# One hybrid decoder block on one core: where weight casts are issued, and how u and y pass through DRAM

## The chip, the core and the metric

The kernel runs on one core of one Trainium2 chip. A core has four compute engines with an instruction queue each: TensorE (PE in the profile; its weight loads are PEld), VectorE (DVE), ScalarE (ACT) and GpSimd (POOL). SyncE (SP) computes nothing here and issues most of the DMAs; ScalarE issues some too. Each queue is worked off in order: an instruction that waits holds up everything behind it on the same engine. The metric is the device time of the whole kernel in microseconds (us). Three runs of the kernel before gave 1589.52, 1594.77 and 1595.97 us, a median of 1594.77.

## The reference, cut to what matters

One layer, 1024 tokens, width 1024, all float32:

```
u = rms_norm(h) ; proj = u @ w_in -> u_ssm, q, k, v, f_logit, gate_logits
y_ssm = gelu(s5_ssm(u_ssm, ...))          # 32 groups of 16 channels, 64 states each
out_a = glu(y_ssm @ w_glu)
out_b = forgetting_attention(q, k, v, f_logit + b_forget) @ w_fox_o      # 8 heads of 64
h = h + (gate_a * out_a + gate_b * out_b) @ w_mix_out
h = h + memory_cross_attention(rms_norm(h), rms_norm(mem), ...)
h = h + (silu(f_a) * f_b) @ w_ffn_out ; out = rms_norm(h)
```

The recurrence of `s5_ssm` is worked in blocks of 8 time steps, so that a group's data has rows of (step within the block, channel of the group), and 128 columns, one for each block.

## The kernel before, in words

Every float32 product is made as three matmuls of a split operand: a rounded copy `hi` (a cast on ScalarE, line 174) and the remainder `lo` (a subtraction on VectorE, line 175). Weights take this way: a DMA into a `raw` buffer (two buffers), the cast into a `whi` buffer and the subtraction into a `wlo` buffer (four each). A `raw` buffer comes free when its subtraction is done, a `whi` buffer when the last matmul that reads it is done. The order of instructions on the engines is not the order of the lines: a scheduler works the program through at build time with a model of durations, and may take an instruction as soon as that model has its inputs and its buffers ready. `B.tc.issue_after(ins)` is the means against it: the instructions of the block that run on the engine of `ins` come behind `ins` in that engine's queue.

The stages, with the times of the profile before:

- **Input** (0 to 111 us): norms, the memory's keys and values, and the projection of `u_ssm` (`ssm_in`, `ssm_out`) in four quarters of 128 channels. `ssm_out` (line 418) copies a quarter to `us`, 128 channels by 8 steps by 128 blocks, and stores it to `u_d` with one DMA for each of its 8 groups (lines 424 and 425).
- **Gates and recurrence** (111 to 327 us, `stage_ssm`): 32 steps `gate(j, h)` of 24 matmuls with a sigmoid on ScalarE, a store to `gate_d` that ScalarE issues (line 462), and the weights of the next gates by `wblock`. Between them, for each quarter q: `turn_weights` (transposes, two copies `F` on ScalarE, seven small DMAs `Ts` <- `W`), `states` (the load of `xg` from `u_d`, line 1346, 16 matmuls of `xg` with `F`, the scan on VectorE), `toeplitz` (one copy `Tt` <- `Ts` on ScalarE, line 1340, placed behind a sigmoid), `out` (16 matmuls, gelu, the split into `yh` and `yl`) and `store` (line 1403: 16 DMAs of 16 partitions each, which bring y to channel rows in `y_d`).
- **Values and first projections** (327 to 396 us): `Fox.prepare_v` loads and splits four blocks of the v weights; `values_of_v` makes v. `project(h)` has a `load` for the q and k weights of head h (two DMAs of 256-byte rows, the cast and the subtraction, lines 1530 to 1543), 16 `part`s of three matmuls, and `evac`.
- **Attention** (396 to 611 us): 8 heads of 12 units (`scores`, an exponential, `values_hi`, `values_lo`). Side work hangs on the units: the parts of head h+2, the row maxima of head h+1, and at unit 5 the `load` of head h+3 (line 1740). In head 6 stand the loads of y from `y_d` (`load_y`), in head 7 the loads of the first `w_glu` weights and their products.
- **Tail** (611 us to the end): the GLU, the mixing projection, cross-attention and the FFN.

## Time and profile before

| | us |
|---|---|
| three runs, median (lowest to highest) | 1594.77 (1589.52 to 1595.97) |
| the profiled execution, its own time | 1596.93 |
| its span, from the first to the last instruction | 1594.9 |
| PE busy in that span | 1537.0 |
| DVE busy | 1021.1 |
| ACT busy | 650.5 |
| POOL busy | 250.1 |

How to read the profile: its first part gives each engine's busy time, the second 40 slices of the span, the fourth the chain of work that ended last. The other views quoted below are answers of the same trace. In a view of stretches, each row has the stretch, its length, the busy time of each engine with the number of its instructions, the TensorE clock that was granted (1.00 is full speed), the share of time in which the DMA engines were busy, and what they moved in GB/s. In a timeline, each row has a start, a duration, the engine, the line, the operation, its output and input, how many instructions were merged, and in brackets how long the engine sat idle before it and what ended that. A row of SPq or ACTq is an instruction that issues a DMA, not the transfer.

### The profile page before, as it was taken

Reading aid. Unit: us, or ns where it says so; the run is one execution under the profiler, and the core shown is the slowest. Engines: PE = TensorE matmul, PEld = TensorE weight load, DVE = VectorE, ACT = ScalarE, POOL = GpSimd, SP = SyncE. Lnnn points to the kernel's source line nnn. Section 1 sums busy time; section 2 is a strip of 40 time slices with the busy share of each in tenths; the row PEclk is TensorE's granted clock in tenths of the full one; section 3 lists DMA queues with packets and bytes.
Section 4 is the critical chain, followed back from the end, with each engine's and each line's share of the span. In section 5 each row is a group of like instructions: output and inputs, shape, how many; then the busy total and the mean of one; then the engine's idle time right before and its main releaser. Section 6 shows DMA issues by size and latency. Waiting matters only on the chain.

```text
span 1594.9 us, 20583 instructions
## 1 busy us (share of the span) xinstructions
PE 1537.0 (96%) x7313; PEld 1263.9 (79%) x7313; DVE 1021.1 (64%) x1850; ACT 650.5 (41%) x1173; POOL 250.1 (16%) x339
## 2 busy tenths in 40 slices
PE   7799999999899999999999989999999999999997
PEld 6588888798677768888888778888888888788886
DVE  6657545345587876766555687776667776565455
ACT  6323434323466653223335564333333333344342
POOL 2026654200121222210002200010000000000001
PEclk8899999999899999999999999999999999999999
DMA  7747455641321526457402186555544444796642
GB/s 265 127 80 135 117 135 98 112 78 24 54 54 49 153 58 201 146 159 268 160 24 97 53 276 232 161 166 160 167 158 152 157 161 152 270 392 224 190 157 106
DMA packets 204278, 236.45 MB, mean 148 GB/s; under 512 B 36984, under 2 KB 133080, under 8 KB 204176
## 3 DMA queue, kind: packets, MB, share of 16 engines
q1 hardware_dynamic: 197552, 219.42, 47.9%
q10 hardware_dynamic: 6624, 15.73, 2.6%
q8 instruction: 57, 0.93, 0.3%
q14 instruction: 45, 0.37, 0.1%
HBM read 161.40 MB, written 71.66 MB: 146 GB/s over the span
## 4 chain that ended last, share of the span: by engine, by line
PE 78%; DVE 7%; DMA 6%; issue 4%; ACT 3%; SPq 1%; POOL 1%; DVEq 0%; POOLq 0%; ACTq 0%
PE mm L858 14%; PE mm L164 7%; PE mm L165 7%; PE mm L166 7%; PE pv L858 7%; PE mm L995 4%; PE sc L858 3%; PE sc L164 3%; PE sc L166 3%; PE sc L165 3%; PE sc L995 3%; PE pv L995 3%; DMA raw<-in_w_in_dram 2%; PE misc L995 1%; DMA xt<-in_x_dram 1%
## 5 line engine op out<-in xcount | busy, mean ns | idle before, releaser
L175 DVE TENSOR_TENSOR wlo<-raw,whi 128x1024 fp32r<-128x1024 f32 (+2 forms) x121 | 130.2, 1077 | 168.4 <-ACT whi L174 167.4
L174 ACT CAST whi<-raw 128x1024 fp32r<-128x1024 f32 (+2 forms) x124 | 112.3, 910 | 225.0 <-DMA raw<-in_w_ffn_in_dram 54.8
L164 PE MATMUL mm<-uh,whi 128*128 128x512 f32 x344 | 138.5, 403 | 0.0
L166 PE MATMUL mm<-uh,wlo 128*128 128x512 f32 x344 | 136.5, 397 | 0.0
L165 PE MATMUL mm<-ul,whi 128*128 128x512 f32 x344 | 136.2, 396 | 0.0
L175 DVE TENSOR_TENSOR ol<-or,oh 128x1024 fp32r<-128x1024 f32 x73 | 89.3, 1223 | 70.9 <-ACT oh L174 69.7
L174 ACT CAST oh<-or 128x1024 fp32r<-128x1024 f32 x73 | 76.8, 1053 | 104.3 <-PE mm L995 35.2
L890 POOL TENSOR_TENSOR g<-a,c 128x512 f32<-128x512 f32 x22 | 35.5, 1613 | 394.8 <-ACT a L889 394.8
L166 PEld LDWEIGHTS mm<-uh,wlo 128*128 128x128 f32 x344 | 65.7, 191 | 13.4 <-DVE wlo L175 0.2
L1625 POOL TENSOR_TENSOR pl<-pf,ph 128x512 fp32r<-128x512 f32 (+1 forms) x32 | 37.3, 1166 | 245.3 <-DVE ph L1624 154.6
L164 PEld LDWEIGHTS mm<-uh,whi 128*128 128x128 f32 x344 | 65.9, 192 | 12.1
L165 PEld LDWEIGHTS mm<-ul,whi 128*128 128x128 f32 x344 | 65.8, 191 | 11.5
L193 POOL TENSOR_TENSOR r<-ms,mhalf 128x1 f32<-128x1 f32 x26 | 15.1, 581 | 356.0 <-DVE ms L189 345.5
L1622 ACT ACTIVATE pf<-sc 128x512 f32<-128x512 f32 (+1 forms) x96 | 46.4, 489 | 52.7 <-DVE sc L1618 32.5
L858 PE MATMUL pv<-S3h,we 128*128 128x512 f32 x176 | 58.1, 389 | 0.0
L995 PE MATMUL mm<-ol,oh 128*128 128x512 f32 x106 | 41.3, 389 | 0.0
L995 PE MATMUL mm<-oh 128*128 128x512 f32 x106 | 41.2, 389 | 0.0
L995 PE MATMUL mm<-oh,ol 128*128 128x512 f32 x106 | 41.2, 389 | 0.0
L1628 DVE TENSOR_TENSOR pl<-pf,ph 128x512 fp32r<-128x512 f32 (+2 forms) x64 | 35.7, 558 | 8.4 <-ACT ph L1627 7.0
L164 PE MATMUL sc<-uh,whi 128*128 128x512 f32 x104 | 40.8, 393 | 0.0
L164 PE MATMUL mm<-yh,whi 128*128 128x512 f32 x104 | 40.8, 392 | 0.0
L165 PE MATMUL mm<-yl,whi 128*128 128x512 f32 x104 | 40.6, 390 | 0.0
(581 smaller groups left out, 4545.6 us busy)
## 6 DMA issues: line engine op xcount, KB each, us to landing
or<-c_d SPq DMA_DIRECT2D x77, 256.0 KB
raw<-in_w_in_dram SPq DMA_DIRECT2D x22, 512.0 KB
wo<-in_w_ffn_out_dram SPq DMA_DIRECT2D x22, 512.0 KB
c_d<-g SPq DMA_DIRECT2D x44, 256.0 KB
t_d<-wo SPq DMA_DIRECT2D x44, 256.0 KB
or<-t_d SPq DMA_DIRECT2D x44, 256.0 KB
raw<-in_w_ffn_in_dram SPq DMA_DIRECT2D x20, 512.0 KB
rawb<-in_w_ffn_in_dram SPq DMA_DIRECT2D x20, 512.0 KB
```

What stands on the lines that cost most here:

```text
L164: T.matmul(ps, lh, rh, start=first, stop=False)
L165: T.matmul(ps, lh, rl, start=False, stop=False)
L166: T.matmul(ps, ll, rh, start=False, stop=last)
L174: self.A.copy(hi, src)
L175: (self.G if pool_lo else self.V).tensor_sub(lo, src, f32(hi))
L193: self.G.tensor_tensor(out=r, in0=v, in1=self.mhalf[:, 0:n], op=ALU.pow)
L858: T.matmul(ps, l_[:, k, :], r_, start=first and k == 0 and i == 0, stop=k == 3 and i == 2, skip_group_check=True)
L890: G.tensor_mul(g[:, 512:], a1, c1)
L995: T.matmul(ps, l_[:, gi], r_[:, 512:], start=n < 3 and p == 0 and k == 0 or n == 7 and p == 0 and k == 0, stop=p == NP - 1 and k == 2, ski ...
L1622: A.activation(pf[:, off:], ps[:, off:], AF.Exp)
L1625: G.tensor_sub(pl[:, off:], pf[:, off:], f32(ph[:, off:]))
L1628: V.tensor_sub(pl[:, off:], pf[:, off:], f32(ph[:, off:]))
```

## The change

There are two parts.

**Casts.** `wload` and `wblock` take an argument `behind`; where it is given, the cast comes behind that instruction on ScalarE. The four v weight blocks are split behind the last `Tt` copy of the recurrence (`B.ordered`). `project(h)` is cut in two: `load` holds the two DMAs alone, and the new `split` (`parted`) makes the cast and the subtraction. In the attention, `load` of head h+3 moves from unit 5 to unit 4, and its `split` stands at unit 9, behind that unit's exponential. For heads 0 to 2 the split stands right behind the load, as before (for head 2 behind a copy of head 1, as before).

**u and y in DRAM.** u is stored with one DMA for a quarter in place of eight, in rows of 4 KB (128 channels by 8 steps by 128 blocks); `xg` is loaded with eight DMAs, one for a group, in place of one. y is stored with one DMA for each of `yh` and `yl` in place of eight, in rows of 4 KB as they lie in SBUF. 64 new DMAs from DRAM to DRAM (`move_y`, 64 KB each in pieces of 512 bytes) bring y to channel rows in `y2_d`; they stand at units 2 to 8 of heads 0 to 4, up to two at a unit. `load_y` reads `y2_d`.

```diff
+    def behind(self, ins):
+        return nullcontext() if ins is None else self.tc.issue_after(ins.ins)
...
-        self.split(hi[:, :cols], lo[:, :cols], raw[:, :cols], pool_lo)
+        with self.behind(behind):
+            self.split(hi[:, :cols], lo[:, :cols], raw[:, :cols], pool_lo)
...
-    u_d = B.dram.tile([GRP, 8, 16, P], F32, name="u_d")
-    y_d = B.dram.tile([2, 512, 8, P], F32, name="y_d")
+    u_d = B.dram.tile([4, P, 8, P], F32, name="u_d")
+    y_d = B.dram.tile([4, 2, P, 8, P], F32, name="y_d")
...
         if h == 1:
-            for g in range(8):
-                S.dma_start(u_d[8 * q + g].rearrange("t n c -> n t c"), uv[16 * g:16 * g + 16])
+            S.dma_start(u_d[q], uv)
...
-        self.B.A.copy(self.Tt.rearrange("p g t m -> p t g m"), self.Ts)
+        self.B.ordered = self.B.A.copy(self.Tt.rearrange("p g t m -> p t g m"), self.Ts)
...
-        S.dma_start(self.xg, u_d[8 * q:8 * q + 8].rearrange("g t n c -> (t n) g c"))
+        for g in range(8):
+            S.dma_start(self.xg[:, g, :], u_d[q, 16 * g:16 * g + 16].rearrange("n t c -> t n c"))
...
         for i, y in enumerate((self.yh, self.yl)):
-            yv = f32(y).rearrange("p (g c) -> p g c", g=8)
-            for t in range(8):
-                self.B.S.dma_start(y_d[i, P * q:P * q + P, t].rearrange("(g m) c -> m g c", m=16),
-                                   yv[16 * t:16 * t + 16])
+            self.B.S.dma_start(y_d[q, i], f32(y).rearrange("p (g c) -> p g c", g=8))
...
-            self.wv[b] = [self.B.wblock(self.w_in, 4 * kk, 4, C_V + c0, n) for kk in range(2)]
+            self.wv[b] = [self.B.wblock(self.w_in, 4 * kk, 4, C_V + c0, n, behind=self.B.ordered) for kk in range(2)]
...
-        def load(behind=None):
+        def load():
...
+        def parted(behind=None):
             wh = B.wpool.tile([P, WSLOT], F32R, tag="whi", name="whi")[:, :D]
             wl = B.wpool.tile([P, WSLOT], F32R, tag="wlo", name="wlo")[:, :D]
-            if behind is None:
-                B.split(wh, wl, raw)
-            else:
-                with B.tc.issue_after(behind.ins):
-                    B.split(wh, wl, raw)
+            with B.behind(behind):
+                B.split(wh, wl, self.raw.pop(h))
...
-        A.activation(pf[:, off:], ps[:, off:], AF.Exp)
+        self.exp = A.activation(pf[:, off:], ps[:, off:], AF.Exp)
...
+        y2_d = B.dram.tile([2, NH * DH, 8, P], F32, name="y2_d")
+
+        def move_y(n):
+
+            q, i, t = n // 16, n // 8 % 2, n % 8
+            S.dma_start(y2_d[i, P * q:P * (q + 1), t].rearrange("(g m) c -> m g c", m=16),
+                        y_d[q, i, 16 * t:16 * (t + 1)])
...
-                            y_d[i, k * P:(k + 1) * P, 4 * h:4 * h + 4, :])
+                            y2_d[i, k * P:(k + 1) * P, 4 * h:4 * h + 4, :])
...
             if h + 3 < NH:
-                side[5].append(pro[h + 3].load)
+                side[4].append(pro[h + 3].load)
+                side[9].append(lambda: pro[h + 3].split(self.exp))
...
+            for n in range(14 * h, min(14 * h + 14, 64)):
+                side[2 + n % 14 // 2].append(lambda n=n: move_y(n))
```

More of the change, by code (lines that the diff above doesn't have):

```diff
@@ L1 @@
 from collections import namedtuple
-from contextlib import ExitStack
+from contextlib import ExitStack, nullcontext
 import concourse.bass as bass
@@ L143, in bank, with wload @@
         return self.psum.tile([P, 512], F32, tag=tag, bufs=self.BANKS[tag], name=tag)
-    def wload(self, pieces, cols, pool_lo=False):
+    def behind(self, ins):
+        return nullcontext() if ins is None else self.tc.issue_after(ins.ins)
+    def wload(self, pieces, cols, pool_lo=False, behind=None):
         raw = self.wpool.tile([P, RAW], F32, tag="raw", bufs=2, name="raw")
@@ L152, in wload, with wblock @@
         lo = self.wpool.tile([P, WSLOT], F32R, tag="wlo", name="wlo")
-        self.split(hi[:, :cols], lo[:, :cols], raw[:, :cols], pool_lo)
+        with self.behind(behind):
+            self.split(hi[:, :cols], lo[:, :cols], raw[:, :cols], pool_lo)
         return hi, lo
-    def wblock(self, w, k0, nk, c0, nc_, pool_lo=False):
+    def wblock(self, w, k0, nk, c0, nc_, pool_lo=False, behind=None):
         src = w[k0 * P:(k0 + nk) * P, c0:c0 + nc_].rearrange("(k p) c -> p k c", p=P)
-        hi, lo = self.wload([(0, (nk, nc_), src)], nk * nc_, pool_lo)
+        hi, lo = self.wload([(0, (nk, nc_), src)], nk * nc_, pool_lo, behind)
         return tuple(t[:, :nk * nc_].rearrange("p (k c) -> p k c", k=nk) for t in (hi, lo))
@@ L1404, in store @@
         for i, y in enumerate((self.yh, self.yl)):
-            yv = f32(y).rearrange("p (g c) -> p g c", g=8)
-            for t in range(8):
-                self.B.S.dma_start(y_d[i, P * q:P * q + P, t].rearrange("(g m) c -> m g c", m=16),
-                                   yv[16 * t:16 * t + 16])
-Projection = namedtuple("Projection", "load parts evac")
+            self.B.S.dma_start(y_d[q, i], f32(y).rearrange("p (g c) -> p g c", g=8))
+Projection = namedtuple("Projection", "load split parts evac")
 class Fox:
@@ L1520, in setup @@
                         channel_multiplier=-1)
-        self.pj, self.mc, self.pvs, self.num, self.rb = {}, {}, {}, {}, {}
+        self.pj, self.mc, self.pvs, self.num, self.rb, self.raw = {}, {}, {}, {}, {}, {}
         self.hi_todo, self.lo_todo = [], []
@@ L1528, in project @@
         K1, K2, Q1, Q2 = self.hb[h % 2]
-        def load(behind=None):
+        def load():
             src = lambda c: self.w_in[:, c + h * DH:c + (h + 1) * DH].rearrange("(k p) c -> p k c", p=P)
-            raw = B.wpool.tile([P, RAW], F32, tag="raw", bufs=2, name="raw")[:, :D]
+            raw = self.raw[h] = B.wpool.tile([P, RAW], F32, tag="raw", bufs=2, name="raw")[:, :D]
             rv = raw.rearrange("p (k c) -> p k c", k=8)
@@ L1563, in evac @@
             return A.copy(K2[64:128, cs], ps[64:128, :])
-        return Projection(load, [lambda hf=hf, k=k: part(hf, k) for hf in range(2) for k in range(8)],
+        return Projection(load, parted, [lambda hf=hf, k=k: part(hf, k) for hf in range(2) for k in range(8)],
                           [lambda: evac(0), lambda: evac(1)])
@@ L1703, in run @@
             pro[h].load()
+            pro[h].split()
         for f in pro[0].parts[:8] + pro[0].evac[:1] + pro[0].parts[8:] + pro[0].evac[1:]:
@@ L1716, in run @@
         self.max_row(0)
-        pro[2].load(copied)
+        pro[2].load()
+        pro[2].split(copied)
         for t in range(5, 7):
```

## The prediction

> **What bounds the kernel now.** I read the page first: the engines' busy time and the chain that ended last.

> ```profile
> span 1594.9 us, 20583 instructions
> PE 1537.0 (96%) x7313; PEld 1263.9 (79%) x7313; DVE 1021.1 (64%) x1850; ACT 650.5 (41%) x1173; POOL 250.1 (16%) x339
> PE 78%; DVE 7%; DMA 6%; issue 4%; ACT 3%; SPq 1%; POOL 1%; DVEq 0%; POOLq 0%; ACTq 0%
> ```

> PE is busy for 96% of the span. The change takes no matmul away, so all it can win is PE's idle time and time at a lowered clock in the stages it touches. Second, the busy time by stage (gates and recurrence; values; attention):

> ```profile
> 111.00:327.00 216.00, 210.93 (x1077) 179.80 (x1076) 112.22 (x150) 79.66 (x124) 104.08 (x206) 0.99 0.60 119
> 327.00:396.00 69.00, 68.04 (x463) 61.99 (x462) 34.33 (x94) 20.00 (x37) 0.00 (x0) 1.00 0.29 41
> 396.00:611.00 215.00, 204.82 (x978) 153.58 (x977) 157.91 (x381) 124.16 (x241) 37.33 (x32) 0.98 0.34 85
> ```

> PE is idle there for 5.1, 1.0 and 10.2 us: 16.3 us in all, the ceiling before clock effects. Third, windows over the stalls themselves; the column after POOL is the granted clock:

> ```profile
> 180.00:187.30 7.30, 7.25 (x40) 5.93 (x39) 0.86 (x2) 0.22 (x1) 5.61 (x8) 1.00 0.95 193
> 187.30:189.80 2.50, 0.03 (x1) 0.03 (x1) 1.13 (x2) 0.67 (x2) 1.32 (x2) 1.00 0.59 116
> 305.90:308.50 2.60, 0.08 (x1) 0.00 (x0) 1.26 (x1) 2.52 (x4) 0.00 (x0) 0.96 0.88 195
> 308.50:311.50 3.00, 2.97 (x14) 2.97 (x15) 0.00 (x0) 1.76 (x2) 0.00 (x0) 0.50 0.76 181
> 401.80:403.80 2.00, 0.12 (x2) 0.07 (x1) 1.68 (x4) 0.56 (x2) 0.00 (x0) 1.00 0.60 87
> 403.80:406.10 2.30, 2.26 (x6) 1.24 (x6) 0.91 (x6) 0.00 (x0) 0.00 (x0) 0.51 0.41 50
> 406.10:408.70 2.60, 0.00 (x0) 0.00 (x0) 0.38 (x1) 1.43 (x2) 0.00 (x0) 0.50 0.96 109
> 408.70:414.10 5.40, 5.37 (x14) 4.21 (x15) 3.12 (x9) 1.37 (x4) 0.73 (x1) 0.50 0.40 55
> ```

> Four holes of about 2.5 us or less, and behind two of the places the clock is at one half. Fourth, what ScalarE did there:

> ```profile
> 189.13 0.59 ACT L1321 COPY F<-pv 128x512 f32<-128x512 f32 x1 [8.91 <-DMA y_d<-yh]
> 301.96 1.08 ACT L174 CAST whi<-raw 128x1056 fp32r<-128x1056 f32 x1 [6.23 <-DMA raw<-in_w_in_dram]
> 305.98 1.07 ACT L174 CAST whi<-raw 128x1056 fp32r<-128x1056 f32 x1 [2.94 <-DMA raw<-in_w_in_dram]
> 306.96 0.59 ACT L461 ACTIVATE gs<-mm 128x512 f32<-128x512 f32 x1
> 307.44 1.03 ACT L1340 COPY Tt<-Ts 128x1024 f32<-128x1024 f32 x1
> 391.06 2.00 ACT L174 CAST whi<-raw 128x1024 fp32r<-128x1024 f32 x2
> 401.04 1.05 ACT L174 CAST whi<-raw 128x1024 fp32r<-128x1024 f32 x1 [2.69 <-DMA raw<-in_w_in_dram]
> 407.24 1.04 ACT L174 CAST whi<-raw 128x1024 fp32r<-128x1024 f32 x1 [4.88 <-DMA raw<-in_w_in_dram]
> 408.19 0.48 ACT L1622 ACTIVATE pf<-sc 128x384 f32<-128x384 f32 x1
> ```

> In three of the places a weight cast waits at the head of ScalarE's queue for a load that has not landed, and the sigmoid, the `Tt` copy and the exponentials that PE needs queue behind it. In the first, at 189.13, the cause differs: ScalarE's own gate store waited for a store of y whose data it does not touch. So in this trace an issue can be held by an older transfer on the other queue.

> **The change part by part.** *The v casts* (1056 columns, so those of lines 1437 and 1438). Their two waits, 6.23 and 2.94 us, come off the path: behind `Tt` they still wait, but the sigmoid and `Tt` have gone, and `out` runs from PE's next free moment. Gain: 2.52 us of idle time (2.60 less 0.08) and half of the 3.0 us at clock 0.50, 1.5: **4.0 us**. The casts keep their cost; the stage that reads their result begins at 327, some 20 us later, which covers two casts and two subtractions. Were that cover gone, the rest of the load would reach PE again: 2.94 us.

> *The q and k casts.* The casts at 401.04 and 407.24 are those of heads 4 and 5 (heads 0 and 1 are cast before PE starts on their parts, heads 2 and 3 at 391.06). Their lines stand in heads 1 and 2; the scheduler took them ahead, as buffers were free. Behind the exponential of unit 9 of those heads they cannot come here. Gain: idle time of 1.88 and 2.60 us, and half of 2.3 and 5.4 us at clock 0.50, 1.15 and 2.70: **8.3 us**. A check from the other side:

> ```profile
> 397.00:430.00 33.00, 28.45 (x129) 21.51 (x129) 17.57 (x46) 14.40 (x29) 4.61 (x4) 0.84 0.43 56
> 435.00:455.30 20.30, 20.23 (x98) 15.17 (x99) 16.88 (x43) 12.92 (x27) 4.59 (x4) 1.00 0.18 41
> ```

> Head 0 takes 33.0 us where head 1 takes 20.3; the extra 31 matmuls are worth some 4, and 8.7 remain. The casts come back inside heads, one cast more than before (that of head 3 was made at 391). The loads then have most of a head to land (25.4 us, from the cast at 455.35 to that at 480.77 below), so the price is the busy time of a cast and a subtraction in a head that idles little: from nothing to their 1.05 and 1.2 us. I take 0.5.

> [...]

> *Loads of w_glu.* `Glu.load` has no `behind`. Before, its casts had to wait for `whi` buffers:

> ```profile
> 432.23 0.94 SPq L150 DMA_DIRECT2D raw<-in_w_glu_dram  x2
> 455.35 1.04 ACT L174 CAST whi<-raw 128x1024 fp32r<-128x1024 f32 x1
> 480.77 1.04 ACT L174 CAST whi<-raw 128x1024 fp32r<-128x1024 f32 x1
> 627.98 0.38 SPq L150 DMA_DIRECT2D raw<-in_w_fox_o_dram  x1
> 634.88 1.05 ACT L174 CAST whi<-raw 128x1024 fp32r<-128x1024 f32 x1 [2.44 <-DMA raw<-in_w_fox_o_dram]
> ```

> 48 us lie between that load and its cast. With the q and k casts later, `whi` buffers are free when w_glu comes, so the cast may again be put too early. Half a megabyte took 6.9 us at 627.98 and held ScalarE 2.44. Bounds: nothing, and as much as the pair at 401 and 407 cost, 8.3. I take 1, since the nearest row's hold of 2.44 us made no hole worth naming.

> *u, y and SyncE.*

> ```profile
> 100.00:110.00 10.00, 10.00 (x46) 8.29 (x45) 0.91 (x1) 1.18 (x2) 3.17 (x7) 1.00 0.27 47
> 110.00:120.00 10.00, 10.00 (x46) 8.29 (x45) 0.00 (x0) 2.98 (x4) 7.25 (x15) 1.00 0.71 119
> ...
> 106.38 11.01 SPq L425 DMA_DIRECT2D u_d<-us  x20
> 176.67 3.09 SPq L150 DMA_DIRECT2D raw<-in_w_in_dram  x2
> 179.81 0.50 SPq L1346 DMA_DIRECT2D xg<-u_d  x1
> 180.36 8.92 SPq L1407 DMA_DIRECT2D y_d<-yh  x8
> 189.38 4.79 SPq L1407 DMA_DIRECT2D y_d<-yl  x8
> 194.28 4.38 SPq L1335 DMA_DIRECT2D Ts<-W  x7
> 200.03 0.94 SPq L150 DMA_DIRECT2D raw<-in_w_in_dram  x2
> ```

> Issues: u 32 to 4, `xg` 4 to 32, y 64 to 8, moves 0 to 64: 8 more in all. At 11.01/20, 0.55 us each, a quarter's y costs SyncE 1.1 us in place of 13.7 (8.92 and 4.79). The removed y and u issues win nothing by themselves: PE is busy throughout 100 to 120, and the one at 187.3 has a second cause behind the first. `xg` was issued at 179.81 behind two raw loads of half a megabyte; 1.5 MB at the 193 GB/s of that window is 8 us, so `xg` lands around 187 to 188, when PE needs it at 187.3. Issued in eight pieces it is complete later, by up to 7 x 0.5 = 3.5 us, less what the backlog hides. So the hole of 2.47 us may go (-2.5) or grow (+3); I take 0. The moves: if they run beside the attention, SyncE has room and the DMA share is 0.18 in head 1; 14 moves are 7.7 us of SyncE in 25 us and 0.9 MB, 5 us at 193 GB/s. Nothing waits for them until `load_y`, whose line stands in head 6, two heads behind the last move, so 0; the other end is the last rival. Their waits are for the stores of y alone; behind one on SyncE could stand the row of maxima that the next head's scores read.

> Sum: -4.0 - 8.3 + 0.5 + 1 + 0 + 0 = **-10.8 us**. The profiled execution took 1596.93 us, 2.0 over its span and 2.2 over the median of the runs; the same sum on it gives 1586.1, and on the median of 1594.8, **1584.0**.

> **The rivals.**

> *A, the hole at 187.3 closes too* and the head boundaries lose some of the casts that stood there: 1584.0 - 2.5 - 0.5 = **1581**. For it: ScalarE's named wait is the old y store. Against it: `xg` lands at the same time.

> *B, the stall moves to the w_glu casts*: 8.3 in place of my 1, 1584.0 + 7.3 = **1591**. For it: four `whi` buffers, and the scheduler put two casts of this size 2.69 and 4.88 us too early. Against it: w_glu comes in rows of 512 bytes, in the middle of a head, with PE behind two score banks.

> [...]

> *D, slower: the moves run among the gates.* They have no buffer to wait for, only the store of y. The load at 432.23 stands on a line of head 7, so the order of lines does not hold the moves back. SyncE then waits for y to land and issues 16 moves, 8.8 us, in each of the first three quarters, and a gate store on ScalarE that is held by one of them stays until it has landed. A hold of 8.91 us cost PE 2.47, so PE rides out 6.4; a hold of 8.91 + 8.8 costs 11.3, and 12.8 with 1.5 of half clock. One such round, 2.5 of it already there, takes 10.3 and nearly cancels the gain; from the second on the kernel is slower: 1584.0 + 2 x 12.8 - 2.5 = **1607**. For it: the wait at 189.13 and the row at 432.23. Against it: the old 16 stores stood at this very place, and only one of their rounds made a hole.

> **How the numbers follow.** Forecast 0.40 (own range 1580 to 1589: the gains less 2.5 for `xg` and nothing for the casts; or with 3 for `xg`, 2.25 for a cast and 1 for w_glu), A 0.10, B 0.16, C 0.10, D 0.24. Faster by over 0.5% (8 us, below 1586.8, about what this measurement can tell) is the forecast and A, 0.50; within it B and C, 0.26; slower D, 0.24. The range of 1577 to 1604 holds all but most of D and a little below A.

> **What would show it.** Right: no cast before the exponential of unit 9 in head 0, head 0 near 22 to 25 us, clock 1.00 from 400 to 415, the last quarter's `Tt` ahead of the v casts, and PE without a hole at 306. For B: ScalarE idle before `whi` with a w_glu load as releaser. [...] For D: issues from `y_d` to `y2_d` before 327 us, with ScalarE idle behind them. The prediction is wrong if the stage to 327 us gets longer, or if the two clock dips stay.

## The result, and the profile after

The changed kernel takes 1604.97 us, the median of six runs (1603.36 to 1608.48); the kernel before took 1594.33 in six runs beside them (1589.52 to 1597.72). The ratio is 1.007, with a 95% interval of 1.0051 to 1.009: slower by 0.7%, where 0.7% faster was forecast. Up to the stage of the gates, lines of the changed kernel lie 3 or 4 further down (the cast is now L178); the lines of the attention have nearly the same numbers in both.

The page of the changed kernel: its span, the engines' busy time, and the chain that ended last.

```profile
span 1602.0 us, 20601 instructions
PE 1541.5 (96%) x7313; PEld 1269.3 (79%) x7313; DVE 1017.9 (64%) x1850; ACT 652.3 (41%) x1173; POOL 256.7 (16%) x339
PE 70%; DVE 11%; DMA 8%; issue 5%; POOL 3%; ACT 3%; SPq 1%; ACTq 0%; DVEq 0%; POOLq 0%
```

In the chain PE has gone from 78% to 70%, DMA from 6% to 8%, DVE from 7% to 11% and POOL from 1% to 3%: the end hangs less often on matmuls. Where, the view of stretches tells (columns as before; the first two rows have the bounds of the gates and the attention in the kernel before, the row of 25.20 us is the first head):

```profile
111.00:327.00 216.00, 206.24 (x1026) 175.61 (x1025) 104.03 (x147) 74.47 (x119) 100.39 (x202) 0.97 0.54 121
396.00:611.00 215.00, 202.07 (x997) 154.10 (x996) 158.03 (x383) 127.84 (x243) 40.59 (x32) 0.98 0.31 74
160.00:170.00 10.00, 7.56 (x38) 6.59 (x37) 6.54 (x8) 6.92 (x9) 7.21 (x24) 0.85 0.29 107
190.00:200.00 10.00, 5.71 (x23) 5.00 (x22) 5.19 (x6) 4.29 (x7) 4.14 (x4) 0.71 0.58 187
310.00:320.00 10.00, 6.97 (x32) 5.85 (x30) 9.87 (x12) 5.24 (x6) 1.65 (x2) 0.86 0.42 133
405.80:431.00 25.20, 25.20 (x132) 19.67 (x131) 16.46 (x46) 13.74 (x28) 4.62 (x4) 1.00 0.07 12
480.00:490.00 10.00, 4.94 (x27) 3.67 (x25) 3.37 (x11) 3.46 (x9) 0.00 (x0) 0.89 0.34 24
490.00:500.00 10.00, 8.29 (x28) 6.68 (x29) 4.28 (x15) 3.45 (x8) 0.74 (x1) 0.60 0.21 34
```

The stall of the first head is gone: it now starts at 405.8, and PE is busy for all of its 25.2 us at clock 1.00. There are holes in three places of the gates (2.44, 4.29 and 2.77 us at the longest, where the kernel before had two of 2.5 and 2.6), and a new one at 480 to 500.

To compare kernels whose stages start at other moments, I use two lengths: from the first to the last sigmoid of the gates, and from the first to the last exponential of the attention. The timeline of ScalarE, before:

```profile
116.65 0.60 ACT L461 ACTIVATE gs<-sc 128x512 f32<-128x512 f32 x1 [3.04 <-PE sc L166]
325.54 0.59 ACT L461 ACTIVATE gs<-mm 128x512 f32<-128x512 f32 x1
397.11 0.60 ACT L1622 ACTIVATE pf<-sc 128x512 f32<-128x512 f32 x1
607.41 0.28 ACT L1622 ACTIVATE pf<-sc 128x128 f32<-128x128 f32 x1 [2.89 <-DVE sc L1618]
```

And of the changed kernel:

```profile
115.69 0.60 ACT L464 ACTIVATE gs<-sc 128x512 f32<-128x512 f32 x1 [2.31 <-PE sc L170]
334.23 0.59 ACT L464 ACTIVATE gs<-mm 128x512 f32<-128x512 f32 x1
405.79 0.60 ACT L1622 ACTIVATE pf<-sc 128x512 f32<-128x512 f32 x1
617.70 0.28 ACT L1622 ACTIVATE pf<-sc 128x128 f32<-128x128 f32 x1 [2.91 <-DVE sc L1618]
```

Gates: 208.9 to 218.5, 9.6 us longer. Attention: 210.3 to 211.9, 1.6 longer. The values between them take 71.6 in both; the start is 1.0 earlier and the stretch behind the last exponential 3.2 shorter. Together +7.0, and the span grew by 7.1 (1594.9 to 1602.0). The stretch behind the last exponential takes from 982.9 to 989.6 us in the eighteen profiles of this case, so a difference of 3.2 us there is not told apart from none.

**The gates.** The timeline of the changed kernel, ScalarE and PE (in brackets the idle time ahead of the row and what ended it), then SyncE's issues:

```profile
152.08 0.74 ACT L1362 COPY zre<-pv 64x256 f32<-64x256 f32 x2 [11.33 <-DMA raw<-in_w_in_dram]
190.68 0.33 ACTq L465 DMA_DIRECT2D gate_d<-gs  x1
191.10 0.60 ACT L464 ACTIVATE gs<-sc 128x512 f32<-128x512 f32 x1 [13.43 <-PE mm L170]
194.26 0.59 ACT L1324 COPY F<-pv 128x512 f32<-128x512 f32 x1 [2.09 <-DMA xg<-u_d]
194.90 3.78 PE L1357 MATMUL pv<-xg,F 128*128 128x128 f32 x16 [4.29 <-ACT F L1324]
303.77 0.74 ACT L1362 COPY zre<-pv 64x256 f32<-64x256 f32 x2 [12.69 <-DMA Ts<-W]
```

```profile
182.01 3.96 SPq L1350 DMA_DIRECT2D xg<-u_d  x4
186.61 0.34 SPq L1409 DMA_DIRECT2D y_d<-yh  x1
189.54 2.49 SPq L1350 DMA_DIRECT2D xg<-u_d  x4
192.13 2.49 SPq L1695 DMA_DIRECT2D y_d<-y_d  x4
...
291.77 12.88 SPq L1338 DMA_DIRECT2D Ts<-W  x7
304.69 9.26 SPq L1695 DMA_DIRECT2D y_d<-y_d  x14
```

The moves (`y_d<-y_d`) run from 192 us on, not beside the attention, and the four last loads of `xg` stand behind a store of y. ScalarE is idle for 11 to 13 us three times. Twice the releaser is a transfer whose data the next instruction doesn't touch: at 303.77 it copies `zre` from `pv`, and what ended its wait is `Ts`. At 191.10 the view names a matmul, but the gate store ahead of that row was issued at 190.68 and its sigmoid had started at 177.07. Each time the instruction that waits is the gate store ahead of the row. In the trace each of the three stores has a wait ahead of it on the semaphore that it signals itself. The program's list of instructions says who else signals that: these are the 5th, 10th and 26th gate store, and eight DMAs ahead of each stands one of SyncE with the same semaphore.

```
ScalarE  L465 DMA gate_d<-gs 128x512 [waits DMAHW1_49,Activation_49]
SyncE    L153 DMA raw<-in_w_in_dram 128x4x256 [waits DMAHW1_49,DVE_49]
ScalarE  L465 DMA gate_d<-gs 128x512 [waits DMAHW3_49,Activation_49]
SyncE    L1350 DMA xg<-u_d 128x1x128 [waits DMAHW3_49]
ScalarE  L465 DMA gate_d<-gs 128x512 [waits DMAHW6_49,Activation_49]
SyncE    L1338 DMA Ts<-W 112x128 [waits DMAHW6_49,DVE_49,Pool_49]
```

In this program the 862 DMAs of SyncE and ScalarE (816 and 46) share eight completion semaphores, DMAHW0 to DMAHW7, handed out in turn in the scheduler's order. In the trace none of the 862 is issued before the last landing of the DMA before it on its semaphore: for the three stores that landing is at 151.63, 190.60 and 303.31, and they are issued at 151.71, 190.68 and 303.38. So here a gate store waits for whatever stood eight DMAs ahead of it in that order. With more small DMAs in the order, the one eight places ahead is a more recent one: by the traces it was issued 10.3 us ahead of the gate store (median of the 32), in the kernel before 13.6.

**The attention.** SyncE's issues at the boundary of heads 2 and 3, the first row of PE behind the hole, and the row of maxima in the chain of waits (start, us from issue to landing):

```profile
480.10 0.37 SPq L1535 DMA_DIRECT2D raw<-in_w_in_dram  x1
481.29 0.70 SPq L1605 DMA_DIRECT2D hb<-mr  x1
482.81 0.40 SPq L1536 DMA_DIRECT2D raw<-in_w_in_dram  x1
491.71 0.80 PE L1615 MATMUL sc<-hb,hb 69*128 69x512 f32 x1 [6.78 <-DMA hb<-mr]
```

```profile
481.29 10.38 DMA hb<-mr
```

The row of maxima, 4 KB, was issued between the two halves of a q and k load and took 10.38 us; PE stood 6.78 us for it. It came in behind the first half: the semaphore of that half counts its last landing at 491.58 us, and the row was there at 491.67. In the kernel before the last q and k load was issued at 409.98, 17.9 us ahead of the next row of maxima (427.89).

### The profile page after: what moved, and what is told of

It reads as the page before. It is cut to its first block, busy times and chain, and to the rows that moved or that the text cites. A ratio compares the mean times of both kernels' runs of the same rounds, so it can differ in the third digit from the quotient of the medians.

```text
span 1602.0 us, 20601 instructions
## 1 busy us (share of the span) xinstructions
PE 1541.5 (96%) x7313; PEld 1269.3 (79%) x7313; DVE 1017.9 (64%) x1850; ACT 652.3 (41%) x1173; POOL 256.7 (16%) x339
## 4 chain that ended last, share of the span: by engine, by line
PE 70%; DVE 11%; DMA 8%; issue 5%; POOL 3%; ACT 3%; SPq 1%; ACTq 0%; DVEq 0%; POOLq 0%
PE mm L861 15%; PE pv L861 7%; PE mm L168 5%; PE mm L170 5%; PE mm L169 5%; PE mm L998 4%; PE sc L861 4%; PE sc L998 3%; PE pv L998 3%; PE sc L168 2%; PE sc L170 2%; PE sc L169 2%; DMA raw<-in_w_in_dram 2%; PE misc L998 1%; PE pv L168 1%
## 5 line engine op out<-in xcount | busy, mean ns | idle before, releaser
L178 ACT CAST whi<-raw 128x1024 fp32r<-128x1024 f32 (+2 forms) x124 | 112.4, 910 | 205.6 <-DMA raw<-in_w_ffn_in_dram 49.6
L178 ACT CAST oh<-or 128x1024 fp32r<-128x1024 f32 x73 | 76.8, 1053 | 103.1 <-PE mm L998 34.9
L1625 POOL TENSOR_TENSOR pl<-pf,ph 128x512 fp32r<-128x512 f32 (+1 forms) x32 | 41.4, 1295 | 242.1 <-DVE ph L1624 219.3
L169 PEld LDWEIGHTS mm<-ul,whi 128*128 128x128 f32 x344 | 65.9, 192 | 11.3
L1622 ACT ACTIVATE pf<-sc 128x512 f32<-128x512 f32 (+1 forms) x96 | 46.6, 490 | 56.5 <-DVE sc L1618 35.6
L170 PE MATMUL sc<-uh,wlo 128*128 128x512 f32 x104 | 41.0, 394 | 0.0
L169 PE MATMUL sc<-ul,whi 128*128 128x512 f32 x104 | 41.0, 394 | 0.0
```

Source lines behind the costliest of these rows:

```text
L169: T.matmul(ps, lh, rl, start=False, stop=False)
L170: T.matmul(ps, ll, rh, start=False, stop=last)
L178: self.A.copy(hi, src)
L1622: self.exp = A.activation(pf[:, off:], ps[:, off:], AF.Exp)
L1625: G.tensor_sub(pl[:, off:], pf[:, off:], f32(ph[:, off:]))
```

## The experiments

Seventeen kernels, the changed one among them, in us; gates and attention are the two lengths defined above, from the profiled execution; each ratio is against runs of the kernel before in the same set. A `diff` below is against the changed kernel; e5, e7, e10, e11, e13 and e15 have u and y as before besides. Gates of the six kernels that have the v casts and the old paths of u and y, with the stores on ScalarE (e1, e5, e9, e10, e11, e13), lie between 204.3 and 206.1, 205.5 on average: differences under some 2 us are not told apart in these lengths. The attention of the three kernels with the old q and k casts (before, e2, e9) lies between 208.4 and 210.8, which says the same of that column.

| | gates | attention | median | ratio to before, 95% interval |
|---|---|---|---|---|
| before | 208.9 | 210.3 | 1594.33 | |
| after | 218.5 | 211.9 | 1604.97 | 1.007 (1.0051 to 1.009) |
| e1_casts | 206.1 | 211.6 | 1590.83 | 0.998 (0.9969 to 0.9991) |
| e2_uy | 218.7 | 208.4 | 1602.26 | 1.0052 (1.004 to 1.0064) |
| e3_moves_held | 210.8 | 223.9 | 1613.07 | 1.0119 (1.0104 to 1.0135) |
| e4_old_u | 210.8 | 211.7 | 1596.13 | 1.0014 (1.0 to 1.0027) |
| e5_order | 206.0 | 211.1 | 1592.42 | 0.9982 (0.9969 to 0.9995) |
| e6_gate_pool | 212.0 | 213.4 | 1599.22 | 1.0031 (1.0018 to 1.0043) |
| e7_best_pool | 216.9 | 211.0 | 1604.81 | 1.0059 (1.004 to 1.0077) |
| e8_all_pool | 210.5 | 212.4 | 1599.01 | 1.0022 (1.0006 to 1.0037) |
| e9_v_only | 205.9 | 210.8 | 1590.87 | 0.9974 (0.9957 to 0.9991) |
| e10_qk_rb | 204.4 | 209.4 | 1588.92 | 0.9969 (0.9953 to 0.9985) |
| e11_qk_pool | 204.3 | 207.9 | 1590.97 | 0.9971 (0.9956 to 0.9985) |
| e12_y_held | 203.8 | 225.8 | 1604.41 | 1.0061 (1.0041 to 1.0081) |
| e13_hold_glu | 206.0 | 206.7 | 1586.31 | 0.9952 (0.9934 to 0.9969) |
| e14_gate_sp | 206.9 | 210.6 | 1593.74 | 1.0004 (0.9991 to 1.0016) |
| e15_best | 207.7 | 203.5 | 1590.35 | 0.9968 (0.9955 to 0.9981) |
| e16_all | 207.2 | 204.7 | 1587.51 | 0.994 (0.9922 to 0.9958) |

### Which part costs the time

**e1_casts**: the changed kernel with u, y and `load_y` as before, no moves.

> The cast part alone, u and y as before. Theory: the casts bring what was forecast for them, 12.3 us, so the last gate sigmoid stands near 322 us (before 325.5), head 0 is short, and the time is 1582 to 1584. The new wait for the row of maxima behind a q and k load (6.8 us of idle time and 3 us of half clock at 485 to 498 in the changed kernel) may come here too: then 1590 to 1593. Rival, that the casts cost the gates their time: last gate sigmoid near 334 and 1600 or more.

**e2_uy**: the changed kernel with the casts as before.

```diff
-            self.wv[b] = [self.B.wblock(self.w_in, 4 * kk, 4, C_V + c0, n, behind=self.B.ordered) for kk in range(2)]
+            self.wv[b] = [self.B.wblock(self.w_in, 4 * kk, 4, C_V + c0, n) for kk in range(2)]
...
-                side[4].append(pro[h + 3].load)
-                side[9].append(lambda: pro[h + 3].split(self.exp))
+                side[5].append(pro[h + 3].load)
+                side[5].append(pro[h + 3].split)
```

> The part on u and y alone, casts as before. Theory: it makes the gates longer by some 10 us through holes near 165, 190 and 315 us, so the last gate sigmoid stands near 335 to 338 and the time is 1604 to 1610, with the two casts of 401 and 407 still there. Rival, that the loss comes of the casts: 1594 to 1596 and a last gate sigmoid near 326.

Gates 206.1 with the casts alone, 218.7 with u and y alone: the loss in the gates belongs to u and y. The casts win 0.2%, with the new hole in their attention (PE idle 6.78 us ahead of 482.60); the forecast for them was 0.7%. The two parts don't add up: alone, in one set of runs, the one wins 3.2 us and the other loses 8.2, and both together lose 10.6. With the gate stores held, the gates take 218.5 with the v casts and 218.7 without, so the gain of the v casts does not arrive, and the attention is 3.5 us longer than in e2.

**e3_moves_held** and **e4_old_u** take one suspect each out of the gates, e3 by this edit:

```diff
-        B.S.dma_start(f32(self.hb[h % 2][2][68:69, :]).rearrange("o (a b) -> o a b", a=NT), f32(mr))
+        self.mrow = B.S.dma_start(f32(self.hb[h % 2][2][68:69, :]).rearrange("o (a b) -> o a b", a=NT), f32(mr))
...
+            with B.tc.issue_after(self.mrow.ins):
+                S.dma_start(y2_d[i, P * q:P * (q + 1), t].rearrange("(g m) c -> m g c", m=16),
+                            y_d[q, i, 16 * t:16 * (t + 1)])
```

and e4, with u stored in eight pieces again, by this one:

```diff
-        for g in range(8):
-            S.dma_start(self.xg[:, g, :], u_d[q, 16 * g:16 * g + 16].rearrange("n t c -> t n c"))
+        S.dma_start(self.xg, u_d[8 * q:8 * q + 8].rearrange("g t n c -> (t n) g c"))
```

> The changed kernel with the 64 moves queued on SyncE behind the row of maxima of their head, so that none runs before the attention. If the moves hold the gate stores: last gate sigmoid back to 322 to 326, 8 to 12 us less, 1592 to 1597. If the eight loads of xg or the stores of y in 4-KB rows hold them: last gate sigmoid stays at 332 to 335 and the time at 1602 to 1606. Moves beside the attention may also delay the row of maxima: then idle time at head boundaries on top.

> The changed kernel with u stored in eight pieces and xg loaded by one DMA as before; y in 4-KB rows and the moves stay. If the eight loads of xg are the holder: the holes near 190 and 315 us go, last gate sigmoid 324 to 328, 1594 to 1599. If the moves are it: last gate sigmoid 332 to 335 and 1602 to 1606.

**e12_y_held** is both edits at once; only the 4-KB stores of y are left among the gates.

> The changed kernel with u and xg as before and the moves queued behind the row of maxima: of the part on u and y, only the stores of y in 4-KB rows stand among the gates. From the first to the last gate sigmoid: before 208.9 us, the cast part alone 206.1, moves among the gates 210.8, eight loads of xg 210.8, both 218.5. Theory, that the two are the holders and the 4-KB stores cost nothing: 203 to 207 us. Rival, that the 4-KB stores hold ScalarE: 210 or more. The moves in the attention cost there what they did with the eight loads of xg (head 0 to head 7 from 399.3 to 623.2, 224 us, where the changed kernel took 212): about 1600 to 1607 in all.

The timeline of e12_y_held, the two sigmoids, and two waits in its attention, of VectorE and of PE:

```profile
116.95 0.60 ACT L465 ACTIVATE gs<-sc 128x512 f32<-128x512 f32 x1 [3.04 <-PE sc L170]
320.78 0.59 ACT L465 ACTIVATE gs<-mm 128x512 f32<-128x512 f32 x1
530.44 1.22 DVE L1668 TENSOR_TENSOR num<-num,rb 64x1024 f32<-64x1024 f32 x1 [7.46 <-DMA rb<-rd_d]
532.05 0.69 PE L1640 MATMUL pv<-ph,vhi 128*65 128x512 f32 x1 [5.88 <-DVE ph L1624]
```

Gates: 203.8 with neither, 210.8 with the moves, 210.8 with the eight loads of `xg`, 218.5 with both. So some 7 us each and 14.7 together (13.0 against the 205.5 of the six kernels above), and the 4-KB stores cost nothing that these lengths show. Neither theory of e3 and e4 that put the loss on one of them alone holds. Held back to the attention the moves cost more than they save: 223.9 against 211.9, 12 us, and 225.8 against the 211.6 of e1, 14. VectorE waits there 13.9 us in six waits for `rb`, the divisors, a transfer of SyncE (1.0 us in the changed kernel), and PE's wait above stands behind one of them. So they were not free there, against the forecast; another place in the attention than behind the row of maxima was not tried.

### Why it costs the time: late data, or a semaphore

**e6_gate_pool** issues the gate stores from GpSimd; in its program they signal eight other semaphores (DMASW0 to DMASW7). **e14_gate_sp** issues them from SyncE, with three `gs` buffers; moves and eight loads stay. The edit of e14 (e6 has `B.G` in the last line, and two buffers):

```diff
-        gs = qp.tile([P, 512], F32, tag="gs", bufs=2, name="gs")
+        gs = qp.tile([P, 512], F32, tag="gs", bufs=3, name="gs")
...
-        A.dma_start(gate_d[j * P:(j + 1) * P, 512 * h:512 * h + 512], gs)
+        S.dma_start(gate_d[j * P:(j + 1) * P, 512 * h:512 * h + 512], gs)
```

> The changed kernel with the 32 gate stores issued by GpSimd in place of ScalarE. In the program every DMA that SyncE or ScalarE issues counts on one of eight completion semaphores in turn, and its issue waits until the DMA before it on that semaphore has landed; DMAs of GpSimd count on others. Theory: this is what holds ScalarE, so its idle times of 11.33, 6.64 and 12.69 us go, the holes near 165, 190 and 315 us shrink, and the stage from the first to the last gate sigmoid takes 205 to 210 us in place of 218.5: 1592 to 1597, with the wait for the row of maxima near 485 still there. Rival, that the transfers themselves come late (xg, Ts, or too much on the DMA engines): the stage stays at 215 to 219 us, 1602 to 1606. GpSimd may lose time in the scan to the stores: up to 5 us of that back.

> The changed kernel with the gate stores issued by SyncE and three gs buffers in place of two; moves and the eight loads of xg stay among the gates. Theory: what costs the 14.7 us of the gates is that ScalarE stands still until a DMA of its semaphore has landed; with the stores on SyncE it stands only when three stores wait, so the stage from the first to the last gate sigmoid takes 205 to 211 us in place of 218.5, and the time is 1592 to 1598. Rival, that xg, Ts and y themselves come too late behind the new issues: 215 us or more, 1602 to 1606.

The timeline of e14_gate_sp, the two sigmoids, and ScalarE's longest wait for a DMA among the gates:

```profile
116.88 0.60 ACT L464 ACTIVATE gs<-sc 128x512 f32<-128x512 f32 x1 [2.31 <-PE sc L170]
184.37 0.60 ACT L464 ACTIVATE gs<-sc 128x512 f32<-128x512 f32 x1 [9.84 <-DMA gate_d<-gs]
323.79 0.59 ACT L464 ACTIVATE gs<-mm 128x512 f32<-128x512 f32 x1
```

206.9 in place of 218.5, with every load of `xg` and 49 of the 64 moves still in that stage. ScalarE still stands 9.84 us there for a free `gs` buffer (the sigmoid writes to one, and its store empties it), but PE rides that out: its only wait of over 1 us in the gates is one of 2.44 us, for `xg`. So the loss was ScalarE held in front of work that PE needs, and late data are at most that one wait. e14 changes two things, the engine and the number of buffers, and three buffers with the stores on ScalarE were not tried; SyncE's order shifts with it too, and the last four loads of `xg` go out at 186.6 in place of 189.5. In e6, with two buffers, only 6.5 of it came back: a store now waits behind the scan on GpSimd, and the sigmoids wait for its buffer, up to 10.9 us. Without the change's DMAs GpSimd is the worse place (**e7_best_pool**: the casts, ordered loads as in e5, stores on GpSimd; 216.9 against 206.0, and 1604.81 us where 1577 to 1581 was expected), and the whole change with both of these repairs is still slower than before (**e8_all_pool**).

> The cast part, the loads in order as in e5_order, the gate stores on GpSimd; u and y as before. Theory: both sets of holes go, the old one at 187 too (2.5 us of idle time, a hold of 8.9 us on ScalarE): 2 to 4 us under e5_order, 1577 to 1581. If GpSimd's stores delay the scan: as e5_order or slower.

> The whole change with both repairs: loads of q and k behind the row of maxima, gate stores on GpSimd. If the two mechanisms are all of the loss: 1605 - 8 to 10 (gates) - 8 to 10 (row of maxima) = 1585 to 1589. If u and y in the new layout cost something beside them: 1592 or more.

### The casts: why their gain did not arrive

**e9_v_only** keeps the v casts alone.

> The kernel before with the v casts behind the last Tt copy and nothing else of the change. Theory: the hole of 2.5 us at 306 and the half clock behind it go and nothing comes in their place; the stage from the first to the last gate sigmoid takes 206 us as in the two kernels that have this edit (before: 208.9), 1590 to 1592. Rival, that the late casts hold up v: the time from the last gate sigmoid to the first exponential grows over the 71.6 us of before, and the time is 1594 or more.

Gates 205.9, 3.0 under before, the time 0.9974 of before, and 71.6 us from the last sigmoid to the first exponential, as before: the late casts hold nothing up. The theory holds.

**e5_order** queues each q and k load behind the row of maxima:

```diff
-                side[4].append(pro[h + 3].load)
+                side[4].append(lambda: pro[h + 3].load(self.mrow))
...
+            with B.behind(behind):
                 S.dma_start(rv[:, :, 0:64], src(C_Q))
                 S.dma_start(rv[:, :, 64:128], src(C_K))
```

> The cast part alone, with the q and k load of head h+3 queued on SyncE behind the row of maxima of head h, so that none of these loads can go out just ahead of a row of maxima. Theory: the hole of 6.78 us before the scores of 482.60 and most of the half clock behind it (windows 465 to 510 lost 6.8 us of PE time and 2 to 4 us of clock) go, and the cast part brings what was forecast for it: 1590.8 - 8 to 10 = 1581 to 1583. Rival, that the row of maxima is slow for another reason (the casts or the two loads of cumulative gates beside it): the hole comes back at this or another head boundary, 1589 to 1592.

The wait for the row of maxima went, and another took its place. The timeline of e5_order, SyncE, DVE and PE:

```profile
494.36 0.40 SPq L1539 DMA_DIRECT2D raw<-in_w_in_dram  x1
494.80 0.58 SPq L1540 DMA_DIRECT2D raw<-in_w_in_dram  x1
498.98 2.44 SPq L1662 DMA_DIRECT2D rc<-num  x1
509.52 0.20 DVE L1663 RECIPROCAL rc<-rc 128x8 f32<-128x8 f32 x1 [6.80 <-DMA rc<-num]
510.54 0.79 PE L1592 MATMUL mm<-hb,hb 68*128 68x512 f32 x1 [5.82 <-DVE mc L1597]
```

Now the divisors of the head before, again 4 KB, come behind the load: the reciprocal waits for them at the head of VectorE's queue, and the maxima that PE needs are queued behind it. No gain, as the rival said, but not for its reason.

**e11_qk_pool** issues the loads of heads 3 to 7 from GpSimd. **e10_qk_rb** queues them behind `rb`, the last small transfer for some 13 us, and casts at unit 11. **e13_hold_glu** adds that the first w_glu loads wait for the row of maxima of head 5.

```diff
+        self.rbd = S.dma_start(rb, self.rd_d[h].partition_broadcast(64))
...
+                side[6 if h else 4].append(lambda: pro[h + 3].load(self.rbd if h else None))
+                side[11 if h else 9].append(lambda: pro[h + 3].split(self.exp))
```

and besides, in e13 (`row5` is the row of maxima of head 5, the second part stands in `wload`):

```diff
+            B.hold = row5 if h == NH - 1 else None
...
+            with self.behind(self.hold):
+                self.S.dma_start(raw[:, off:off + n].rearrange("p (k c) -> p k c", k=shape[0]), src)
```

> The cast part, with the q and k loads of heads 3 to 7 issued by GpSimd, so on another queue than the row of maxima. If the small transfer is late because it stands behind the load in the same queue: no wait of PE for the row of maxima over 2 us, 1581 to 1586. If it is late because the DMA engines are taken by the 256-byte rows whatever the queue: the wait of 6.8 us stays, 1589 to 1593.

> The cast part, with the q and k load of heads 4 to 7 queued on SyncE behind the last small transfer of the divisors (rb), where for some 11 us no transfer on the path follows, and its cast at unit 11. Theory: a q and k load takes some 11 us in 256-byte rows, and every small transfer of SyncE that comes behind it within that time is late (the row of maxima in the changed kernel, the divisors in e5_order). Then no hole over 2 us is left at any head boundary from 395 to 530 and the time is 1581 to 1585. Rival, that small transfers are late for another reason: a hole of 5 to 7 us comes back, 1589 to 1593. The cast at unit 11 may come too early for its load: then ScalarE idle before it, some 2 us a head.

> As e10_qk_rb, and the first w_glu loads queued on SyncE behind the row of maxima of head 5, so that the q and k load of head 7 (issued at 507.2, landed at 523.6, with a w_glu load behind it) has the DMA engines to itself. Theory: the wait of 2.65 us before the cast at 523.63 and the hole of 2.78 us with its half clock go, 3 to 5 us under e10_qk_rb: 1584 to 1587. Rival, that the hole moves on to the w_glu casts or the loads of y of heads 6 and 7: no gain, 1588 to 1591.

The issues of e11_qk_pool at a boundary of heads, on SyncE and GpSimd, and the wait of PE behind them:

```profile
469.30 0.70 SPq L1609 DMA_DIRECT2D hb<-mr  x1
469.38 0.90 POOL L1539 DMA_DIRECT2D raw<-in_w_in_dram  x1 [2.69 <-DVE mr L1608]
470.06 0.41 SPq L1575 DMA_DIRECT2D hb<-cum_d  x1
479.01 0.30 PE L1592 MATMUL mm<-hb 68*128 68x128 f32 x1 [4.34 <-DMA hb<-cum_d]
```

The row of maxima is in time, but it was issued 0.08 us ahead of the load, so this does not show that another queue would have saved it. The next small transfer of SyncE (`cum_d`, 8 KB), issued 0.68 us behind the load on GpSimd, came 8.8 us after its issue, and PE stood 4.34 us for it: a queue of its own for the load did not keep it from delaying a small transfer, and the time is that of e1 (1590.97 and 1590.83 us).

In e10_qk_rb PE waited nowhere over 1 us from 395 to 520, as expected; the time, 1588.92, stayed above the 1581 to 1585 that were expected with it. Behind 520, a wait of ScalarE and PE:

```profile
523.63 1.04 ACT L178 CAST whi<-raw 128x1024 fp32r<-128x1024 f32 x1 [2.65 <-DMA raw<-in_w_in_dram]
524.73 0.51 PE L168 MATMUL mm<-uh,whi 128*128 128x512 f32 x1 [2.78 <-ACT whi L178]
```

That load, issued at 507.20, had a w_glu load behind it. With that held back (e13) the wait of the cast is 0.44 us, the attention takes 206.7 us and the kernel 0.9952 of before (0.9969 in e10; the two intervals overlap). This is the prediction's rival B in part: with the casts later, w_glu loads come where they disturb.

### Both causes taken away

**e15_best** is e13 with the gate stores of e14; **e16_all** is the whole change with the edits of e10, e13 and e14.

> As e13_hold_glu, with the gate stores issued by SyncE and three gs buffers: u and y as before. Theory: the hold of 8.72 us on ScalarE that ends at 189.28 goes, and with it the hole of 2.32 us, so the stage from the first to the last gate sigmoid takes 202 to 205 us in place of 206.0, and the time is 1582 to 1585. Rival, that xg is complete no earlier (in e14_gate_sp PE still waited 2.44 us for it): 205 to 207 us and 1585 to 1588.

> The whole change, both parts, with the gate stores on SyncE, the q and k loads behind rb and the w_glu loads behind the row of maxima of head 5. If the shared semaphores and the small transfers behind the q and k loads are all that went wrong: the stage of the gates as in e14_gate_sp (206.9), the attention as in e13_hold_glu (206.7), 1585 to 1589. If 4-KB rows and moves bring something of their own: 1584 or less. If the moves cost in the attention too: 1591 or more.

e16_all, the change in full, takes 1587.51 us, 0.994 of before; the changed kernel took 1.007. Its gates are 207.2 and its attention 204.7. With both causes taken away (and the w_glu loads in order) the change is within 3.5 us of the 1584 that was forecast. Whether the part on u and y then gains anything of its own is not shown: without it e15_best took 1590.35 in the same set (0.9955 to 0.9981, which just meets the 0.9922 to 0.9958 of e16), but e13_hold_glu, also without it, is at 0.9952, and the gates of e13, e15 and e16 (206.0, 207.7, 207.2) are not told apart. e15 missed its theory: the hold of 8.72 us on ScalarE went, but PE then waited 3.86 us for `xg` itself, so at 187 us `xg` was the second cause, as the prediction had said. Its 1590.35 us lie above both its theory (1582 to 1585) and its rival (1585 to 1588).

## Why the prediction was wrong

Two steps failed: the two zeros for `xg` and the moves, which cost the gates some 7 us each, and the gain of the q and k casts, which a late row of maxima took back. The sign of being wrong that the prediction named came true: the stage of the gates got longer.

**The v casts, -4.0**: right in kind and about in size. e9_v_only shows 3.0 us in the gates and 4.0 us in the time. In the changed kernel they do not arrive, as the held stores set the length of the gates.

**The q and k casts, -8.3 + 0.5, and w_glu +1**: the holes at 401 and 407 went as forecast, and with nothing in the way the attention takes 203.5 to 206.7 us (e15, e16, e13) in place of 210.3: 3.6 to 6.8, where the terms give 6.8. What failed is the step "The loads then have most of a head to land". It asked only whether the load would be in time for its cast. A moved load brings its transfer along, and the question is what stands behind that transfer: a row of maxima with no slack at all. The text had named that row, "behind one on SyncE", but for the moves alone. In the changed kernel this took back all of the gain (211.9 us in place of 210.3).

**`xg`, 0 (-2.5 to +3)**: some +7. The step counted the issue time of eight loads and their landing. It left out the other stores and loads in the turn of semaphores, though the trace of before showed the mechanism: a gate store held by a store of y that it does not touch. I read that row as "an older transfer on the other queue" and took it for one event instead of asking by what rule a store is held.

**The moves, 0 if beside the attention**: both halves failed. They ran among the gates and cost some 7 us there, and held to the attention they cost 12 to 14.

**Rival D** had the place right (moves among the gates, ScalarE's store held, loss of the size of two rounds, 1607), but for a reason that was only half of it: SyncE's wait for y is not what decides, and the eight loads cost as much as the moves. That its 1607 is close to the 1604.97 measured is luck: it kept the whole gain of the casts, which did not arrive, and took two rounds of 12.8 us for a loss of 13 to 15 in the gates. It got 0.24; the "for it" row, a load taken a whole head early, should have weighed more, since no line of the change ties the moves to the attention. **C**, a loss by the eight loads of `xg` themselves: no run shows such a term. In e14 the eight loads stand among the gates and these take 206.9 us, against 207.7 without them in e15. In the trace the semaphore of each of the eight loads at 182 to 192 us counts nine landings, the first 1.0 to 1.8 us behind the issue and eight late ones, where that of the one load before (at 179.81) counted sixteen; what that does to their time is not shown. **A**: the hole of before at 187.3 had `xg` as a second cause, as e15 shows.

## What to carry to other kernels

Before adding small DMAs, find out what a DMA's issue waits for besides its data, and keep issues off an engine whose queue holds work on the path: the same transfers cost 13 to 15 us with the gate stores on ScalarE (218.5 against 203.8 to 205.5) and nothing that shows with the stores on SyncE and a third buffer (206.9 and 207.2 against 207.7). When a bulk load is moved, look for the small transfers issued in the ten microseconds behind it (two of those took 10.38 and 8.8 us here) and which engine waits for them with nothing to spare (PE, 6.78 and 4.34 us). Where order matters, tie it to an instruction: the scheduler does not take the place of a line in the program as a promise.

## What was not expected of the hardware

Two q and k loads of the same shape move at very different rates. Stretches of one us of the changed kernel, two beside the load issued at 429.19 and three in the wait of PE behind 484.9 (the last three columns are the clock, the DMA share and GB/s):

```profile
433.00:434.00 1.00, 1.00 (x8) 0.91 (x6) 0.93 (x3) 0.62 (x2) 0.00 (x0) 1.00 0.62 87
434.00:435.00 1.00, 0.58 (x5) 0.28 (x3) 0.00 (x0) 0.98 (x2) 0.00 (x0) 1.00 0.71 98
...
485.00:486.00 1.00, 0.00 (x0) 0.00 (x0) 0.00 (x0) 0.81 (x2) 0.00 (x0) 1.00 0.46 25
486.00:487.00 1.00, 0.00 (x0) 0.00 (x0) 0.00 (x0) 0.00 (x0) 0.00 (x0) 1.00 0.35 25
490.00:491.00 1.00, 0.00 (x0) 0.00 (x0) 0.00 (x0) 0.00 (x0) 0.00 (x0) 0.50 0.79 112
```
